# Other rotary groups, and exchanged rows for the layer norm, in a planned two-layer encoder

## The chip, the cores and the metric

The kernel runs on one core of a Trainium2 chip. The metric is the device time of one execution in microseconds (us), taken as the median of several runs. The engines are PE (matrix products; PEld loads their stationary operand), DVE (vector work), ACT (activations and copies), POOL and SP. SP issues almost all DMAs, in the order of its program; POOL issues those that add into memory. Every engine runs its own instructions strictly in the order in which they were written down, so an instruction that waits holds everything behind it on that engine.

## The reference

Two layers over 512 positions of width 1024. Each layer has a token mixer and a squared-ReLU MLP, and each of these four sub-layers is wrapped alike (shift, scale and gate come from the conditioning vector c):

```python
h = x * (1 + scale) + shift
x = layer_norm(DN_ALPHA * x + (1 + gate) * f(h), ln_g, ln_b)
```

The mixer of layer 0 is windowed attention with 8 query heads and 2 key heads (head h uses key head h // 4), with rotary embedding on the first 32 of 128 dimensions:

```python
qkv = h @ w_in
q, k = partial_rope(q, cos, sin), partial_rope(k, cos, sin)
scores = einsum(qb, kb) * HEAD_DIM ** -0.5        # band of 3 blocks of 128
probs = softmax with a sink logit per head
o = einsum(probs, vb) @ w_out
```

The mixer of layer 1 is a recurrent block.

## The kernel before, in words

The kernel is written as a list of operations in program order (`Program.add`). Then `Program.schedule` plans them: it runs through time with a cost for each operation, keeps for each engine the operations whose inputs are done, and takes the one of lowest priority number (its place in the list, shifted by hand-set offsets). What comes out is one fixed order for each engine, and the eight PSUM banks are dealt out along with it. So a change in what waits for what changes the order of many instructions, not only of those in the diff. All of them carry line 502 in the profile (500 for the transposes that open a tile); tiles are told apart by name.

Matrix products are done in three passes (`mm3`): every operand is split into a high part and a rest. Weights come from HBM into four buffers `raw`, ACT casts the high part into one of six buffers `w`, and DVE subtracts to get the rest. `hth` and `htl` hold the layer's input, split and transposed.

In `attn`, after the projection, eight PSUM tiles hold k0, k1 and q0 to q5. `rope` takes four of them at a time: ACT copies the first 32 rows of each into a packed 128-row buffer in `rows[4]`, the tiles are copied whole to their places, DVE shuffles, multiplies by the tables of cosines and sines in `rows[2]`, and adds, and SP sends the four rotated pieces back by DMA. It is called for k0, k1, q0, q1, then for q2 to q5, and later for q6 and q7, always with `rows[4]`. The names of the copies in memory: k0 and k1 are `hid_106` and `hid_107`, q0 is in `exa`, q1 in `ex_73` (profile: `ex`), q3 in `ex_74`, q4 in `exb`, q5 in `ex_75` (profile: `ex`).

Then come the heads in the order 0, 5, 1, 2, 3, 4, 6, 7 (function `head`): four score products, a masking step with a maximum on DVE, exponentials on ACT, normalising, ten transposes on PE, copies, four products with V. Between the heads' instructions PE does the late projection of q6 and q7 (`w_91`, `w_92`) and the first output products.

Behind all this run the background products with the conditioning weights (`gemv_tasks`): `exc`, `hida` and, later, `htl` and `exa`, `exb` are loaded with 128 rows of a weight, scaled and summed over eight such loads. In the first of these products every other load is scaled on ACT and added by a DMA that POOL issues (`rows<-exc`); the others are added on DVE. A buffer is loaded anew when its rows have been added.

`load_ln_rows` loads the layer norm's g into `rows[1]` and b into `rows[2]`. `mod_rows` multiplies (1 + scale) by g into `rows[3]` and scales g and b by alpha. `evac` adds an output tile to x, `ln_block` normalises a block of 128 positions, transposes it, and at the end multiplies x by g on DVE and adds b by a DMA from POOL. Memory is shared: `rows[0]` holds c until the projection is done and the gate row later; `rows[1]` also holds two of the eight score buffers of the heads (`srings`) and, in the first MLP, every other sum of the background products; `rows[2]` also holds the rotary table; in the recurrent block both are parts of larger buffers.

Of the kernel before, what the change touches and what calls it, by code (L numbers as in the profile page):

```python
# [12 lines left out]
ALU = mybir.AluOpType  # L13
# [538 lines left out]
class Kernel:  # L552
# [143 lines left out]
    def fill(self):  # L696
# [17 lines left out]
        QE='aavavavava',  # L714
# [100 lines left out]

    def load_ln_rows(self, i):
        nc = self.nc
        nc.sync.dma_start(out=self.rows[1][:, :], in_=self.I["lng"][i].partition_broadcast(128))
        nc.sync.dma_start(out=self.rows[2][:, :], in_=self.I["lnb"][i].partition_broadcast(128))

    def mod_rows(self, ln, shift, scale):

        nc, v = self.nc, self.nc.vector
        r = self.rows
        v.scalar_tensor_tensor(out=r[3][:, :], in0=r[3][:, :], scalar=1.0, in1=r[1][:, :], op0=ALU.add, op1=ALU.mult)
        for i in (1, 2):
            nc.scalar.activation(out=r[i][:, :], in_=r[i][:, :], func=AF.Copy, scale=ALPHA)
        self.renew("ex", (8, 9))
        sel, tmp = r[4][0:36, 0:512], [self.acc2[0:4, i * 256 : i * 256 + 256] for i in range(3)]
        nc.sync.dma_start(out=sel, in_=self.I["sel"])  # L830
        nc.scalar.copy(out=self.ex[9][0:36, :].bitcast(F32R), in_=sel)
        nc.sync.dma_start(out=tmp[0], in_=self.I["lnb4"][ln])
        for i, row in ((1, scale), (2, shift)):
            nc.sync.dma_start(out=tmp[i].rearrange("p (f c) -> p f c", f=2), in_=self.mods[row][0:1, :].quarters())
        v.scalar_tensor_tensor(out=tmp[1], in0=tmp[1], scalar=1.0, in1=tmp[0], op0=ALU.add, op1=ALU.mult)
        v.tensor_tensor(out=tmp[2], in0=tmp[2], in1=tmp[1], op=ALU.add)
        nc.gpsimd.memset(self.ex[8][0:36, 0:256], 0.0)
        nc.scalar.copy(out=self.ex[8][0:4, 0:256].bitcast(F32R), in_=tmp[2])
        v.tensor_tensor(out=self.ex[8][32:36, 0:256].bitcast(F32R), in0=tmp[2], in1=self.ex[8][0:4, 0:256], op=ALU.subtract)
# [23 lines left out]
    def ln_block(self, t, last=False, parts=1):  # L863
        nc = self.nc
        v = nc.vector
        end = last and t == TB - 1
        near = last and t == TB - 2
        xs = self.xb[t][:, :]
        mv = self.small("mv", 8)
        v.bn_aggr(out=mv[:, 0:2], in_=self.st[t][:, :].rearrange("p (a b) -> p a b", a=2 * parts))  # L870
        nc.scalar.activation(out=mv[:, 2:3], in_=mv[:, 1:2], func=AF.Sqrt, bias=self.eps[:, 0:1])
        v.tensor_scalar(out=mv[:, 3:4], in0=mv[:, 1:2], scalar1=EPS, scalar2=None, op0=ALU.add)
        v.reciprocal(out=mv[:, 4:5], in_=mv[:, 2:3])
        if not end:
            v.scalar_tensor_tensor(out=mv[:, 7:8], in0=mv[:, 0:1], scalar=-1.0, in1=mv[:, 4:5], op0=ALU.mult, op1=ALU.mult)
        v.scalar_tensor_tensor(out=mv[:, 5:6], in0=mv[:, 4:5], scalar=mv[:, 3:4], in1=mv[:, 4:5], op0=ALU.mult, op1=ALU.mult)
        v.tensor_scalar(out=mv[:, 5:6], in0=mv[:, 5:6], scalar1=-0.5, scalar2=1.5, op0=ALU.mult, op1=ALU.add)
        v.tensor_tensor(out=mv[:, 6:7], in0=mv[:, 4:5], in1=mv[:, 5:6], op=ALU.mult)
        mu, rstd = mv[:, 0:1], mv[:, 6:7]
        if not end:  # L880
            v.tensor_tensor(out=mv[:, 7:8], in0=mv[:, 7:8], in1=mv[:, 5:6], op=ALU.mult)
        for fh in range(2):
            c = slice(fh * 512, fh * 512 + 512)
            xh = xs[:, c]
            u = self.ex[8 + 2 * (t & 1) + fh][:, :]
            h = self.ex[4 * (t & 1) + 2 * fh][:, :]
            if end or near and not fh:
                v.scalar_tensor_tensor(out=u, in0=xh, scalar=mu, in1=self.rows[1][:, c], op0=ALU.subtract, op1=ALU.mult)
                w = 256 if end and fh else 512
                for i in range(0, 512, w):  # L890
                    b = slice(fh * 512 + i, fh * 512 + i + w)
                    v.scalar_tensor_tensor(
                        out=h[:, i : i + w], in0=u[:, i : i + w], scalar=rstd, in1=self.rows[2][:, b], op0=ALU.mult, op1=ALU.add
                    )
                    nc.sync.dma_start(out=self.O[t * 128 : t * 128 + 128, b], in_=h[:, i : i + w])
            elif last:
                nc.scalar.activation(out=xh, in_=xh, func=AF.Identity, scale=rstd, bias=mv[:, 7:8])
                nc.gpsimd.tensor_tensor(out=u, in0=xh, in1=self.rows[1][:, c], op=ALU.mult)
                nc.gpsimd.tensor_tensor(out=h, in0=u, in1=self.rows[2][:, c], op=ALU.add)
                nc.sync.dma_start(out=self.O[t * 128 : t * 128 + 128, c], in_=h)  # L900
            else:
                nc.scalar.activation(out=xh, in_=xh, func=AF.Identity, scale=rstd, bias=mv[:, 7:8])
                v.tensor_tensor(out=h, in0=xh, in1=self.rows[3][:, c], op=ALU.mult)
            if last:
                continue
            pt = self.ps()
            for j in range(4):
                nc.tensor.transpose(pt[:, j * 128 : j * 128 + 128], h[:, j * 128 : j * 128 + 128], self.ident[:, :], start=j == 0)
            bm, sel = self.ex[8][0:36, fh * 128 : fh * 128 + 128].bitcast(F32R), self.ex[9][0:36, :].bitcast(F32R)
            nc.tensor.matmul(pt[:, :], lhsT=bm, rhs=sel, start=False, stop=True, skip_group_check=True)  # L910
            a = fh * 2048
            hv, lv = (x[:, a : a + 2048].rearrange("p (k n) -> p k n", k=4)[:, :, t * 128 : t * 128 + 128] for x in self.ht)
            pv = pt[:, :].rearrange("p (k n) -> p k n", k=4)
            if self.par("LE") == "v":
                self.split(pv, hv.bitcast(F32R), lv.bitcast(F32R))
            else:
                uv = u.rearrange("p (k n) -> p k n", k=4)
                nc.scalar.copy(out=hv.bitcast(F32R), in_=pv)
                nc.scalar.copy(out=uv, in_=pv)
                nc.gpsimd.tensor_tensor(out=lv.bitcast(F32R), in0=uv, in1=hv, op=ALU.subtract)  # L920
        if not last:
            self.nc.offset += self.par("XO")
            e = v if self.par("XE") == "v" else nc.gpsimd
            e.tensor_tensor(out=xs, in0=xs, in1=self.rows[1][:, :], op=ALU.mult)
            nc.gpsimd.dma_start(out=xs, in_=self.rows[2][:, :], accum_op=ALU.add)
            self.nc.offset -= self.par("XO")

    def warm_sqrt(self):
# [109 lines left out]
        nc.sync.dma_start(out=self.rows[2][:, :], in_=I["rope"].rearrange("p a b -> p (a b)"))  # L1038
        nc.sync.dma_start(out=self.ex[12][:, 0:384], in_=I["mask"])

    def rope(self, heads, how):

        nc, v = self.nc, self.nc.vector
        n = 32 * len(heads)
        cos, sin = self.rows[2][:n, 0:512], self.rows[2][:n, 512:1024]
        pk, sw = self.rows[4][:n, 0:512], self.rows[4][:n, 512:1024]
        for i, (p, dst) in enumerate(heads):
            nc.scalar.copy(out=self.rows[4][32 * i : 32 * i + 32, 0:512], in_=p[0:32, :])
        for i, (p, dst) in enumerate(heads):
            if how[i] == "a":  # L1050
                nc.scalar.copy(out=dst, in_=p[:, :])
            else:
                v.tensor_copy(out=dst, in_=p[:, :])
        v.stream_shuffle(out=sw, in_=pk, mask=[(i + 16) % 32 for i in range(32)])
        v.tensor_tensor(out=pk, in0=pk, in1=cos, op=ALU.mult)
        v.tensor_tensor(out=sw, in0=sw, in1=sin, op=ALU.mult)
        v.tensor_tensor(out=pk, in0=pk, in1=sw, op=ALU.add)
        for i, (p, dst) in enumerate(heads):
            nc.sync.dma_start(out=dst[0:32, :], in_=self.rows[4][32 * i : 32 * i + 32, 0:512])

    def attn(self):
        nc, I = self.nc, self.I
        v = nc.vector
# [12 lines left out]
        def KTt(kv, lo, hi):  # L1076
            return hid[8 + kv][:, lo:hi]
# [86 lines left out]
        self.own = self.big[:2]  # L1164
        self.modes = self.P["AM"]
        qk = [(tiles[m], KTt(m, 0, 512) if m < 2 else Q(m - 2, 0, 512)) for m in range(8)]
        self.rope(qk[:4], self.P["QE"][:4])
        self.rope(qk[4:], self.P["QE"][4:8])
        accv, r = self.acc2, [a[:, :] for a in self.rows]
        self.bgq += self.gemv_tasks(0, 2, r[3], self.rows[0], red="pe", ap=self.P["AP0"])  # L1170
        self.bgq += self.gemv_tasks(1, 1, accv, self.rows[3], red="pe", ap=self.P["AP1"])
# [2 lines left out]
        u = N_WQ  # L1174
        self.prep(u + 1, ahead=2)
        self.nc.offset += self.P["VP"]
        for t in range(TB):
            p = self.ps()
# [15 lines left out]
        for n in range(2):  # L1194
            u = N_WQ + 2 + n
            self.prep(u, ahead=2)
            p = self.ps()
# [405 lines left out]
```

## Time and profile before

| | us |
|---|---|
| median of 3 runs (1181.89 to 1183.45) | 1182.77 |
| time of the profiled execution | 1187.53 |
| span of its trace | 1185.7 |
| PE busy in that span | 1146.8 |
| DVE busy | 822.9 |
| ACT busy | 530.3 |
| mean granted clock of PE | 0.988 |

The trace belongs to one execution, so durations are compared with its own time. A row of the timeline gives start, duration, engine, operation, output and inputs, shape, and in brackets how long the engine was idle before and what ended that. "Granted clock" is the share of PE's full clock that it was given.

### The profile page before, as it was taken

To read this page: it belongs to the slowest core of one execution; us is meant where nothing else is said; L and a number is where in the kernel's file an instruction comes from. 1 tells how busy PE (TensorE), PEld (TensorE's weight loads), DVE (VectorE), ACT (ScalarE), POOL (GpSimd) and SP (SyncE) were. 2 spreads that over 40 slices of the span, in tenths; PEclk is the share of its full clock that TensorE was granted. 3 is DMA by queue.
4 is the path that set the end of the run, shared out by engine and by line. 5 is a ranking of instruction groups with operands and counts; after the bars stand their busy time and mean duration, and the time that the engine had idled before them with its cause. 6 is when DMAs were issued, how large, how long until landed. Compare 5 with 4: busy or idle time off the path is not lost.

```text
span 1185.7 us, 14389 instructions
## 1 busy us (share of the span) xinstructions
PE 1146.8 (97%) x5292; PEld 932.8 (79%) x5292; DVE 822.9 (69%) x1228; ACT 530.3 (45%) x784; POOL 100.6 (8%) x73
## 2 busy tenths in 40 slices
PE   6989999999999999999999999999999999999995
PEld 4876677988888888888887877878988888888884
DVE  8767878898999844448748889799644444444447
ACT  5357554521332522324469989825422422422411
POOL 1000000233222200000000000000000000000004
PEclk9989999999999999999999999999999999999998
DMA  9876754876588332223434464544722223222201
GB/s 347 320 213 184 260 171 127 255 258 246 188 318 313 102 112 89 99 98 74 134 106 127 143 157 125 154 148 140 199 89 100 96 89 107 89 95 101 89 1 72
DMA packets 57369, 181.85 MB, mean 153 GB/s; under 512 B 8017, under 2 KB 8589, under 8 KB 57298
## 3 DMA queue, kind: packets, MB, share of 16 engines
q1 hardware_dynamic: 53698, 170.19, 41.5%
q0 software_dynamic: 3600, 10.75, 4.9%
q8 instruction: 41, 0.67, 0.2%
q14 instruction: 30, 0.25, 0.1%
HBM read 160.29 MB, written 2.13 MB: 137 GB/s over the span
## 4 chain that ended last, share of the span: by engine, by line
PE 70%; DVE 11%; ACT 8%; DMA 7%; issue 3%; SPq 0%; DVEq 0%; ACTq 0%
PE ps L502 69%; DVE w L502 3%; ACT rows L502 3%; DVE rows L502 2%; ACT w L502 2%; ACT L502 1%; DMA rows<-rows 1%; DMA raw<-in_W 1%; DVE ex L502 1%; PE ps L500 1%; DVE acc L502 1%; DVE xb L502 1%; DMA rows<-w 1%; ACT ex L502 1%; ACT acc L502 1%
## 5 line engine op out<-in xcount | busy, mean ns | idle before, releaser
L502 PE MATMUL ps<-hth,w 128*128 128x512 f32 (+1 forms) x1776 | 505.4, 369 | 2.8 <-ACT hth L502 1.8
L502 DVE TENSOR_TENSOR w<-raw,w 128x1024 fp32r<-128x1024 f32 x192 | 236.9, 1238 | 240.5 <-ACT w L502 238.4
L502 ACT CAST w<-raw 128x1024 fp32r<-128x1024 f32 x192 | 198.4, 1040 | 431.0 <-PE ps L502 382.6
L502 PEld LDWEIGHTS ps<-hth,w 128*128 128x128 f32 x1776 | 321.8, 190 | 61.8 <-ACT hth L502 1.9
L502 PE MATMUL ps<-w,hid 128*128 128x512 f32 (+1 forms) x1581 | 368.9, 390 | 0.0
L502 PEld LDWEIGHTS ps<-w,hid 128*128 128x128 f32 x1581 | 295.1, 189 | 64.4 <-issue 0.7
L502 PE MATMUL ps<-htl,w 128*128 128x512 f32 (+1 forms) x888 | 326.8, 368 | 0.0
L502 PEld LDWEIGHTS ps<-htl,w 128*128 128x128 f32 x888 | 168.1, 189 | 29.4 <-issue 0.7
L502 PE MATMUL ps<-w,hth 128*128 128x512 f32 (+1 forms) x256 | 68.4, 373 | 2.8 <-DVE w L502 1.7
L502 DVE SCALAR_TENSOR_TENSOR ex<-rows,ps 128x512 f32<-128x512 f32 (+1 forms) x81 | 53.2, 674 | 13.8 <-PE ps L502 13.7
L502 DVE TENSOR_TENSOR ex<-rows 128x512 f32<-128x512 f32 x64 | 48.6, 761 | 10.8 <-ACT rows L502 10.7
L502 DVE TENSOR_TENSOR xb<-xb,ex 128x512 f32<-128x512 f32 (+1 forms) x81 | 54.9, 694 | 1.4 <-ACT xb L502 0.9
L502 PEld LDWEIGHTS ps<-w,hth 128*128 128x128 f32 x256 | 45.3, 188 | 13.0 <-DVE w L502 2.1
L502 PE MATMUL ps<-w,hida 128*128 128x512 f32 (+1 forms) x219 | 54.2, 388 | 0.0
L502 ACT ACTIVATE rows<-ps 128x512 f32<-128x512 f32 x66 | 39.1, 593 | 25.8 <-PE ps L502 25.8
L502 DVE TENSOR_TENSOR hid<-ex,hid 128x512 fp32r<-128x512 f32 x57 | 45.5, 797 | 3.9
L502 PEld LDWEIGHTS ps<-w,hida 128*128 128x128 f32 x219 | 40.9, 188 | 8.8
L502 ACT ACTIVATE hid<-rows 128x512 fp32r<-128x512 f32 x56 | 35.4, 632 | 1.7
L502 POOL DMA_DIRECT2D xb<-rows x12 | 10.5, 874 | 290.7 <-DVE xb L502 157.4
L502 ACT ACTIVATE xb<-xb,mv 128x512 f32<-128x512 f32 x29 | 22.1, 809 | 29.0 <-DVE mv L502 29.0
L502 ACT ACT_TABLE_LOAD x26 | 33.4, 1283 | 3.2 <-DMA w<-w 2.1
L502 POOL TENSOR_TENSOR ex<-xb,rows 128x512 f32<-128x512 f32 x3 | 3.8, 1286 | 329.5 <-ACT xb L502 329.5
(191 smaller groups left out, 1020.0 us busy)
## 6 DMA issues: line engine op xcount, KB each, us to landing
raw<-in_W SPq DMA_DIRECT2D x184, 512.0 KB
exc<-in_adaw SPq DMA_DIRECT2D x28, 512.0 KB
exa<-in_adaw SPq DMA_DIRECT2D x19, 512.0 KB
exb<-in_adaw SPq DMA_DIRECT2D x18, 512.0 KB
xb<-rows POOLq DMA_DIRECT2D x12, 512.0 KB, 5.3
hida<-in_adaw SPq DMA_DIRECT2D x9, 512.0 KB
ex<-in_ada0t SPq DMA_DIRECT2D x17, 256.0 KB
htl<-in_adaw SPq DMA_DIRECT2D x6, 512.0 KB
```

The costliest lines, as they stand in the source:

```text
L500: op.ins = nc.tensor.matmul(args[0], lhsT=args[1], rhs=args[2], is_transpose=True, stop=False, skip_group_check=True, **kw)
L502: op.ins = getattr(getattr(nc, op.eng), op.fn)(*args, **kw)
```

## The change

Two things. The first call of `rope` takes k0, k1, q0 and q5, with `rows[4]` as before; the second takes q1 to q4 and packs them into `rows[0]`. And g is loaded into `rows[2]`, b into `rows[1]`, with every use of the two following.

```diff
     def load_ln_rows(self, i):
         nc = self.nc
-        nc.sync.dma_start(out=self.rows[1][:, :], in_=self.I["lng"][i].partition_broadcast(128))
-        nc.sync.dma_start(out=self.rows[2][:, :], in_=self.I["lnb"][i].partition_broadcast(128))
+        nc.sync.dma_start(out=self.rows[2][:, :], in_=self.I["lng"][i].partition_broadcast(128))
+        nc.sync.dma_start(out=self.rows[1][:, :], in_=self.I["lnb"][i].partition_broadcast(128))
...
-        v.scalar_tensor_tensor(out=r[3][:, :], in0=r[3][:, :], scalar=1.0, in1=r[1][:, :], op0=ALU.add, op1=ALU.mult)
-        for i in (1, 2):
+        v.scalar_tensor_tensor(out=r[3][:, :], in0=r[3][:, :], scalar=1.0, in1=r[2][:, :], op0=ALU.add, op1=ALU.mult)
+        for i in (2, 1):
...
-            e.tensor_tensor(out=xs, in0=xs, in1=self.rows[1][:, :], op=ALU.mult)
-            nc.gpsimd.dma_start(out=xs, in_=self.rows[2][:, :], accum_op=ALU.add)
+            e.tensor_tensor(out=xs, in0=xs, in1=self.rows[2][:, :], op=ALU.mult)
+            nc.gpsimd.dma_start(out=xs, in_=self.rows[1][:, :], accum_op=ALU.add)
...
-    def rope(self, heads, how):
+    def rope(self, heads, how, at=4):
...
-        pk, sw = self.rows[4][:n, 0:512], self.rows[4][:n, 512:1024]
+        pk, sw = self.rows[at][:n, 0:512], self.rows[at][:n, 512:1024]
...
-        self.rope(qk[:4], self.P["QE"][:4])
-        self.rope(qk[4:], self.P["QE"][4:8])
+        self.rope(qk[:3] + qk[7:], self.P["QE"][:4])
+        self.rope(qk[3:7], self.P["QE"][4:8], 0)
```

The plan comes out differently from the rotary step to the first part of the first MLP; further on only a few row loads and scalings change places. Three places follow, each before and after.

PE, after the V products: `hid_106` and `hid_107` are the keys k0 and k1, `ex_73` is q1, `ex_75` is q5, `w_91` is a weight of the late projection. Before:

```order
L502 MATMUL ps_687<-hid_106,ex_73 128x256
L502 MATMUL ps_691<-hid_106,ex_73 128x384
L502 MATMUL ps_697<-hid_106,ex_73 128x384
L502 MATMUL ps_702<-hid_106,ex_73 128x256
L502 MATMUL ps_705<-hth,w_91 128x512
L502 MATMUL ps_705<-htl,w_91 128x512
L502 MATMUL ps_705<-hth,w_91 128x512 x2
...
L502 MATMUL ps_718<-hid_107,ex_75 128x256
L502 MATMUL ps_720<-hid_107,ex_75 128x384
```

After:

```order
L502 MATMUL ps_684<-hid_106,exa 128x384
L502 MATMUL ps_688<-hid_106,exa 128x256
L502 MATMUL ps_690<-hid_107,ex_75 128x256
L502 MATMUL ps_693<-hid_107,ex_75 128x384
L502 MATMUL ps_696<-hid_107,ex_75 128x384
L502 MATMUL ps_700<-hid_107,ex_75 128x256
L502 MATMUL ps_703<-hid_106,ex_73 128x256
L502 MATMUL ps_707<-hid_106,ex_73 128x384
L502 MATMUL ps_711<-hid_106,ex_73 128x384
L502 MATMUL ps_720<-hid_106,ex_73 128x256
L502 MATMUL ps_722<-hth,w_91 128x512
```

Head 5's scores now come directly behind head 0's; before, head 1's and the first seven matmuls of the late projection stood between.

ACT, the copies out of PSUM after the projection: `ps_190` to `ps_240` are k0, k1, q0 to q5, and `exc` is the first load of the background products. Before:

```order
L502 CAST w_92<-raw_85 128x1024
L502 COPY ex_73<-ps_201 128x512
L502 COPY ex_74<-ps_227 128x512
L502 COPY ex_75<-ps_240 128x512
L502 ACTIVATE exc<-exc,sc 128x1024
L502 CAST w_87<-raw_82 128x1024
L502 COPY hid_109<-ps_537 128x256
L502 CAST w_88<-raw_83 128x1024
L502 COPY hid_110<-ps_573 128x256
L502 COPY rows<-ps_204 32x512
```

After:

```order
L502 CAST w_92<-raw_85 128x1024
L502 COPY rows<-ps_204 32x512
L502 COPY rows<-ps_240 32x512
L502 COPY ex_75<-ps_240 128x512
L502 COPY rows<-ps_227 32x512
L502 COPY rows<-ps_233 32x512
L502 COPY exa<-ps_204 128x512
L502 COPY exb<-ps_233 128x512
L502 CAST w_87<-raw_82 128x1024
L502 CAST w_88<-raw_83 128x1024
L502 COPY hid_109<-ps_536 128x256
L502 ACTIVATE exc<-exc,sc 128x1024
```

The packing of q2 to q5 has moved ahead, and the scaling of `exc` behind it, two casts and a V copy.

SP, the loads at the end of the heads: `rows<-in_lng` is g, `rows<-in_lnb` is b, `xb` are the four blocks of x. Before (b is loaded much earlier, right behind the rows of q6 and q7):

```order
L502 DMA mods_1244<-rows 1x1024
L502 DMA raw_85<-in_W 128x1024
L502 DMA xb_1294<-in_x 128x1024
L502 DMA rows<-in_sel 36x512
L502 DMA raw_82<-in_W 128x1024
L502 DMA rows<-in_lng 128x1024
L502 DMA mods_1327<-acc_69 1x1024
L502 DMA xb_1332<-in_x 128x1024
```

After (g is in that earlier place):

```order
L502 DMA mods_1254<-rows 1x1024
L502 DMA rows<-in_lnb 128x1024
L502 DMA xb_1279<-in_x 128x1024
L502 DMA xb_1287<-in_x 128x1024
L502 DMA xb_1291<-in_x 128x1024
L502 DMA xb_1296<-in_x 128x1024
L502 DMA raw_85<-in_W 128x1024
L502 DMA rows<-in_sel 36x512
```

The late row is now b, and it stands ahead of all four blocks of x and of two weight loads.

More of the change, by code (lines that the diff above doesn't have):

```diff
@@ L887, in ln_block @@
             if end or near and not fh:
-                v.scalar_tensor_tensor(out=u, in0=xh, scalar=mu, in1=self.rows[1][:, c], op0=ALU.subtract, op1=ALU.mult)
+                v.scalar_tensor_tensor(out=u, in0=xh, scalar=mu, in1=self.rows[2][:, c], op0=ALU.subtract, op1=ALU.mult)
                 w = 256 if end and fh else 512
@@ L892, in ln_block @@
                     v.scalar_tensor_tensor(
-                        out=h[:, i : i + w], in0=u[:, i : i + w], scalar=rstd, in1=self.rows[2][:, b], op0=ALU.mult, op1=ALU.add
+                        out=h[:, i : i + w], in0=u[:, i : i + w], scalar=rstd, in1=self.rows[1][:, b], op0=ALU.mult, op1=ALU.add
                     )
@@ L897, in ln_block @@
                 nc.scalar.activation(out=xh, in_=xh, func=AF.Identity, scale=rstd, bias=mv[:, 7:8])
-                nc.gpsimd.tensor_tensor(out=u, in0=xh, in1=self.rows[1][:, c], op=ALU.mult)
-                nc.gpsimd.tensor_tensor(out=h, in0=u, in1=self.rows[2][:, c], op=ALU.add)
+                nc.gpsimd.tensor_tensor(out=u, in0=xh, in1=self.rows[2][:, c], op=ALU.mult)
+                nc.gpsimd.tensor_tensor(out=h, in0=u, in1=self.rows[1][:, c], op=ALU.add)
                 nc.sync.dma_start(out=self.O[t * 128 : t * 128 + 128, c], in_=h)
@@ L1045, in rope @@
         cos, sin = self.rows[2][:n, 0:512], self.rows[2][:n, 512:1024]
-        pk, sw = self.rows[4][:n, 0:512], self.rows[4][:n, 512:1024]
+        pk, sw = self.rows[at][:n, 0:512], self.rows[at][:n, 512:1024]
         for i, (p, dst) in enumerate(heads):
-            nc.scalar.copy(out=self.rows[4][32 * i : 32 * i + 32, 0:512], in_=p[0:32, :])
+            nc.scalar.copy(out=self.rows[at][32 * i : 32 * i + 32, 0:512], in_=p[0:32, :])
         for i, (p, dst) in enumerate(heads):
@@ L1058, in rope @@
         for i, (p, dst) in enumerate(heads):
-            nc.sync.dma_start(out=dst[0:32, :], in_=self.rows[4][32 * i : 32 * i + 32, 0:512])
+            nc.sync.dma_start(out=dst[0:32, :], in_=self.rows[at][32 * i : 32 * i + 32, 0:512])
     def attn(self):
```

## The prediction

> **What bounds the kernel now.** I read the page first: the shares of the engines and the chain that ended last.
>
> ```profile
> span 1185.7 us, 14389 instructions
> PE 1146.8 (97%) x5292; PEld 932.8 (79%) x5292; DVE 822.9 (69%) x1228; ACT 530.3 (45%) x784; POOL 100.6 (8%) x73
> PE 70%; DVE 11%; ACT 8%; DMA 7%; issue 3%; SPq 0%; DVEq 0%; ACTq 0%
> ```
>
> PE is busy for 97% of the span and has 70% of the chain. The change adds and removes no matmul, so it can only win where PE waits or runs at a lower clock. The instruction order (below) shows which stretches it touches: from the rotary step, at about 57 us, to the first quarter of the first MLP. From there on PE's order is the same. So next I read the windows of that stretch; the columns are the stretch, its length, busy time of PE, PEld, DVE, ACT and POOL, the granted clock, and the DMA share.
>
> ```profile
> 72.00:83.00 11.00, 6.68 (x28) 4.45 (x26) 6.95 (x16) 7.49 (x16) 0.87 (x1) 0.94 0.92 280
> 83.00:95.00 12.00, 12.00 (x43) 8.70 (x44) 7.10 (x24) 5.28 (x12) 0.00 (x0) 0.77 0.34 103
> 95.00:160.00 65.00, 62.77 (x271) 43.97 (x270) 54.78 (x116) 43.04 (x107) 2.66 (x3) 1.00 0.68 222
> 185.00:215.00 30.00, 29.74 (x181) 24.49 (x181) 25.53 (x52) 13.56 (x21) 3.91 (x5) 0.94 0.61 161
> ```
>
> PE is idle for 4.3 us in the first and 2.2 us in the third. In the second it is busy throughout, but 23% of its clock is withheld: 0.23 x 12 = 2.8 us. In the last it is 0.06 x 30 = 1.8 us. PE's timeline and the transfers name the waits:
>
> ```profile
> 72.26 2.31 PE L502 MATMUL ps<-hid,exa 128*128 128x256 f32 x8
> 77.48 0.50 PE L502 MATMUL ps<-hth,w 128*128 128x512 f32 x1 [0.75 <-DVE mx L502]
> 82.93 4.61 PE L502 MATMUL ps<-hid,ex 128*128 128x256 f32 x8 [3.57 <-issue]
> 90.60 0.38 PE L502 MATMUL ps<-ident,xb 128*128 128x128 f32 x2
> 77.73 0.59 SPq L502 DMA_DIRECT2D ex<-rows  x1
> 66.14 4.64 DMA exa<-rows
> ```
>
> At 72.26 head 0's scores start, at 90.60 its first transposes. Between them PE stands for 3.57 us before head 5's scores (82.93). Head 5's query is q5, whose rotary rows went out last of the second group, on SP at 77.73; another row DMA of that kind took 4.64 us (the chain's row at 66.14), so these landed at about 82.4. The wait is for q5.
>
> The second place is the first layer norm.
>
> ```profile
> 159.91 0.27 PE L502 MATMUL ps<-ident,rows 128*128 128x128 f32 x1
> 160.21 5.62 DMA rows<-in_lng
> 165.92 1.23 DVE L502 SCALAR_TENSOR_TENSOR rows<-rows 128x1024 f32<-128x1024 f32 x1 [1.97 <-DMA rows<-in_lng]
> 167.18 1.06 ACT L502 ACTIVATE rows<-rows 128x1024 f32<-128x1024 f32 x1 [3.96 <-DVE rows L502]
> 170.03 2.01 ACT L502 ACTIVATE xb<-xb 128x1024 f32<-128x1024 f32 x2
> 167.35 2.27 PE L502 MATMUL ps<-w,hid 128*128 128x512 f32 x9
> 169.45 1.55 PE L502 MATMUL ps<-w,hth 128*128 128x512 f32 x6
> 185.00 0.63 PE L500 MATMUL ps<-ident,exa 128*128 128x128 f32 x4 [1.17 <-DVE exa L502]
> ```
>
> The last head's transposes read `rows[1]` at 159.91; only then may g be loaded into it. DVE waits for g (165.92), ACT behind DVE (167.18), the evacuations behind both, and PE stands 1.17 us for the first normalised block (185.00).
>
> **Part one, the rotary groups.** With q5 in the first group, head 5's scores follow head 0's, and seven late projection matmuls no longer come between. The 3.57 us go, and with them the low clock behind them, 2.8 us: 6.3 us, if PE's next work is ready. It isn't quite.
>
> ```profile
> 57.95 1.78 ACT L502 COPY rows<-ps 32x512 f32<-32x512 f32 x3
> 61.66 1.57 ACT L502 COPY ex<-ps 128x512 f32<-128x512 f32 x3
> 63.10 1.19 ACT L502 ACTIVATE exc<-exc,sc 128x1024 f32<-128x1024 f32 x1
> 64.15 1.08 ACT L502 CAST w<-raw 128x1024 fp32r<-128x1024 f32 x1
> 70.87 1.18 ACT L502 COPY rows<-ps 32x512 f32<-32x512 f32 x2 [1.30 <-DMA exa<-rows]
> 70.59 1.28 DVE L502 SCALAR_TENSOR_TENSOR rows<-hida,sc,rows 128x1024 f32<-128x1024 f32 x1 [2.88 <-DMA rows<-exc]
> 70.58 0.33 SPq L502 DMA_DIRECT2D exc<-in_adaw  x1
> 75.34 1.15 ACT L502 ACTIVATE exc<-exc,sc 128x1024 f32<-128x1024 f32 x1 [0.74 <-DMA exc<-in_adaw]
> 79.14 0.30 ACT L502 ACTIVATE es<-nm,sinks 128x4 f32<-128x4 f32 x1 [1.35 <-DVE nm L502]
> 81.43 0.19 ACT L502 ACTIVATION_READ_ACCUMULATOR ex<-ex,nm 128x1 f32 x1
> 89.19 0.15 DVE L502 TENSOR_TENSOR den<-den,es 128x4 f32<-128x4 f32 x1
> ```
>
> Before, the second group's packing waited on ACT for the first group's row DMAs (70.87). Now it doesn't, so four row copies and all of the head copies are drawn ahead of the first gate-row scaling `exc`, with two weight casts and one V copy. By their rows (0.59, 0.53 and about 1.0 us apiece, the V copy, half as wide as a head's, put at 0.3) that scaling starts at 61.7 + 4 x 0.59 + 3 x 0.53 + 2 x 1.0 + 0.3 = 67.9 us, 4.8 us later than 63.10; 61.66 is where the copies after the last common cast began. Everything in its loop moves along: its add by DMA landed at 70.5 (DVE's wait at 70.59), SP reloaded `exc` at 70.58, ACT could scale again at 75.34. Now that second scaling comes at about 80.1, and on ACT it stands ahead of head 0's exponentials. These began 3.8 us after it (79.14), of which 1.35 were a wait for DVE that is over by then: 80.1 + 2.5 = 82.6. They take until 82.6 + 2.5 = 85.1 (79.14 to 81.62). From the sum on DVE (89.19) to the transposes (90.60) it was 1.4 us: 86.5 instead of 90.60.
>
> PE is there by then or soon after: three heads' scores (2.3 us each) from 72.26 end at 79.2, and 18 matmuls at 0.233 us (167.35 to 169.45 for 9) end at 83.4, or at 87.6 with the whole burst at half clock. So head 0's transposes come 4.1 us earlier, with one matmul less done (0.2): 3.9. The bounds are 2.8 (half clock) and 6.3 (nothing waits). Head 5's transposes then find ACT still busy with head 0's copies and a cast; I give back 0.7 us, between 0 and the 1.2 of one such scaling. Net **-3.2 us**. What could cost here and is covered is on DVE:
>
> ```profile
> L502 DVE TENSOR_TENSOR w<-raw,w 128x1024 fp32r<-128x1024 f32 x192 | 236.9, 1238 | 240.5 <-ACT w L502 238.4
> ```
>
> The first group's shuffle now stands behind one more weight step (1.2 us), so its rows go out that much later and `exa` lands at 72.0 instead of 70.8; PE wants it at 72.26. If that cover is gone, PE waits for the difference, and a wait of a few tenths is what I would expect at worst. On SP the rows of q1 to q4 go out behind one weight load; head 1's scores, third on PE, want q1 at 72.26 + 2 x 2.3 = 76.9, so its rows must leave by 72.3, and packing that no longer waits (70.87) allows that.
>
> **Part two, g and b.** `rows[2]` is free after the last rotary group, so g loads during the heads and the multiplication by it no longer holds the evacuations: 1.97 + 1.23 = 3.2 us of the chain. PE's order puts the first transposes 6 matmuls (1.4 us) earlier. 3.2 - 1.4 covers the 1.17 us wait with 0.6 to spare. Now b is the late row: SP holds it until the last head's transposes, and all four loads of x stand behind it. From 159.91 the last x was scaled at 172.04, 12.1 us. But PE's order now has 50 matmuls (11.7 us), not 21, and the last head's product between these transposes and the end of the first output half, so x is ready about there. I take -1.17 and -1.8 for the clock behind it: **-3.0 us**, between 0 and -3.0.
>
> The half clock is taken from these rows: 1.17 us of waiting, then
>
> ```profile
> 187.00:188.00 1.00, 1.00 (x4) 0.87 (x4) 0.70 (x2) 0.59 (x1) 0.60 (x1) 0.70 0.00 0
> 190.00:191.00 1.00, 1.00 (x5) 0.77 (x4) 0.68 (x3) 0.52 (x1) 0.00 (x0) 0.59 1.02 197
> ```
>
> a clock below 1 from 187 to 191 with PE busy. The Trainium skill, "TensorE: Matmul & The Clock Gate", section "Why this matters for your kernels", says that PE falls back to half clock after a wait of over some 3 us. The trace has the fall after 1.17 us; by that rule the 1.8 us would stay and part two be worth 1.2 us.
>
> **Where the rows swap later.**
>
> ```profile
> 777.62 0.33 SPq L502 DMA_DIRECT2D rows<-in_lnb  x1
> 781.37 1.06 ACT L502 ACTIVATE rows<-rows 128x1024 f32<-128x1024 f32 x1 [0.21 <-DMA rows<-in_lnb]
> 783.90 1.22 DVE L502 SCALAR_TENSOR_TENSOR rows<-rows 128x1024 f32<-128x1024 f32 x1
> 220.04 0.33 SPq L502 DMA_DIRECT2D rows<-in_lnb  x1
> 231.80 3.26 DVE L502 SCALAR_TENSOR_TENSOR rows<-exb,sc,rows 128x1024 f32<-128x1024 f32 x1
> ```
>
> After the recurrent block `rows[2]` comes free later than `rows[1]`; g now goes out at 777.62 in b's place and lands at 781.3, the multiplication begins at 783.90: nothing, with 2.5 us in reserve. In the first MLP `rows[1]` is a sum row of the background products. It must now wait for the adds of b, which ended before 220.04 (b's load waited for them); a clearing and a bias load follow, and the first sum in it was at 231.80: nothing.
>
> **The sum.** -3.2 - 3.0 = -6.2 us. The profiled execution, 1187.53 us by its own time (span 1185.7), becomes 1181.3. It ran 4.8 us above the median of the three runs, 1182.77; against that the forecast is 1182.77 - 6.2 = **1176.6 us**.
>
> **Rivals.**
> - One gain only: the heads give theirs back later, or the layer norm still waits. 1182.77 - 3.1 = 1179.7. For it: DVE has 54.8 of 65 us in the heads, so little is idle.
> - The clock behind 185.00 falls for another reason and stays: -4.4, 1178.4. Against it: the clock is 1.00 from 95 to 160, where no such wait stands, and fell behind both longer ones. This is what the skill's rule would make of it.
> - Nothing: q5's place is taken by the scaling on ACT, landing some 4 us later than I count, and b takes g's: 1182.8.
> - Slower: DVE becomes the bound of the heads. The new order ends the heads 29 matmuls (6.8 us) earlier in PE's stream, and DVE's idle time there is 10.2 us, of which PE's earlier arrival takes 3 to 4. If DVE holds PE at the transposes of the six later heads, each wait of 1.17 us costs 1.8 more in clock, 3.0 us; the third takes -6.2 to +2.8: 1185.6. It decides from the third such wait on. Against it: no wait of PE between 95 and 160 lowered the clock, and the sums of the background products moved behind the heads in DVE's order.
>
> **How the numbers follow.** Forecast 0.52 (its own range 1174 to 1179.5), one gain 0.18, the clock 0.05, nothing 0.12, slower 0.13. The low end: all idle time and lost clock of the four windows (4.3 + 2.8 + 2.2 + 0.3 + 1.8) and the 1.17 make 12.6, so 1170.2 is the floor; I put 1171. The high end, 1183.5, takes in "nothing" and leaves out most of "slower". A measurement of this kernel can tell 0.2% (2.4 us) from no change. Faster by more: the forecast, the clock case and 0.13 of "one gain", 0.70. Within: 0.05 + 0.12 = 0.17. Slower: 0.13.
>
> **What would show it.** Right: head 5's scores directly behind head 0's on PE, no wait of over 1 us and no clock of 0.5 for 5 us in 79 to 89; `exc` scaled near 68 and 80; head 0's transposes near 86.5; DVE's multiplication by g without a wait for its load; PE's first transposes of the layer norm without a wait, and a clock of 1.00 behind them. Wrong: transposes of head 0 near 90, or waits of over 1 us before several heads' transposes with half clock behind each, or ACT waiting for b.

## The result, and the profile after

The changed kernel is slower: 1191.66 us (median of 5 runs, 1188.02 to 1192.43) against 1183.45 us in the same job, a ratio of 1.0054 (95% interval 1.0028 to 1.0080). A second job gave 1190.67 us and 1.0043 (1.0019 to 1.0066). Three executions in all the jobs (1418 us of the kernel before, 1523 of swap_first_norm below, 2929 of the changed kernel) lay far above the rest and are left out of every ratio. The forecast was 1176.6 us. The profiled execution took 1192.43 us, with a span of 1190.7.

The page after, span and busy time; before, PE had the same work in a span 5 us shorter:

```profile
span 1190.7 us, 14377 instructions
PE 1147.0 (96%) x5292; PEld 934.0 (78%) x5292; DVE 821.9 (69%) x1228; ACT 530.6 (45%) x784; POOL 100.8 (8%) x73
```

The windows of the changed stretch (columns as in the prediction; the last two are the first MLP's beginning):

```profile
72.00:83.00 11.00, 8.82 (x35) 6.18 (x34) 7.48 (x21) 4.58 (x8) 0.87 (x1) 1.00 0.95 286
83.00:95.00 12.00, 11.29 (x53) 7.65 (x52) 8.83 (x25) 10.92 (x30) 0.85 (x1) 1.00 0.56 151
95.00:160.00 65.00, 62.48 (x266) 43.85 (x265) 52.08 (x109) 43.24 (x101) 1.81 (x2) 1.00 0.78 253
185.00:215.00 30.00, 29.10 (x211) 25.71 (x210) 23.20 (x42) 13.05 (x19) 2.57 (x3) 1.00 0.74 199
215.00:240.00 25.00, 21.19 (x129) 18.61 (x128) 23.92 (x25) 11.18 (x16) 9.26 (x4) 1.00 0.63 205
240.00:262.00 22.00, 20.78 (x84) 16.95 (x85) 21.05 (x17) 6.37 (x7) 8.31 (x3) 0.92 0.85 309
```

In these windows of the heads and of the layer norm the clock is 1.00, and PE is idle for 2.2 us in the first window where it was 4.3. But from 215 to 240 us, where PE had been busy for all 25 us, it now stands for 3.8. PE's timeline names the places:

```profile
74.04 2.75 PE L502 MATMUL ps<-hid,ex 128*128 128x256 f32 x10
78.96 1.99 PE L502 MATMUL ps<-hid,ex 128*128 128x384 f32 x6 [2.17 <-DVE mx L502]
85.51 0.44 PE L502 MATMUL ps<-ident,xb 128*128 128x128 f32 x2 [0.43 <-DVE xb L502]
178.31 0.66 PE L500 MATMUL ps<-ident,exa 128*128 128x128 f32 x4
204.12 0.63 PE L500 MATMUL ps<-ident,exb 128*128 128x128 f32 x4 [0.90 <-DVE exb L502]
235.11 1.08 PE L502 MATMUL ps<-w,hid 128*128 128x512 f32 x4
241.22 1.00 PE L502 MATMUL ps<-hth,w 128*128 128x512 f32 x2 [5.04 <-DVE w L502]
571.29 0.63 PE L500 MATMUL ps<-ident,exb 128*128 128x128 f32 x4 [1.66 <-DVE exb L502]
```

Head 0's transposes stand at 85.51 (before 90.60), the layer norm's first at 178.31 without a wait (before 185.00 with 1.17 us), its last at 204.12; before, these stood at 211.68, as this row shows, and those of the second layer norm at 571.15:

```profile
211.68 0.55 PE L500 MATMUL ps<-ident,exb 128*128 128x128 f32 x3 [0.25 <-DVE exb L502]
571.15 0.63 PE L500 MATMUL ps<-ident,exb 128*128 128x128 f32 x4 [1.66 <-DVE exb L502]
```

One sign that the prediction had named for being wrong did appear: ACT waited 3.93 us for b. PE lost nothing by it, as its first transposes (178.31) show.

```profile
153.29 1.06 ACT L502 ACTIVATE rows<-rows 128x1024 f32<-128x1024 f32 x1 [3.93 <-DMA rows<-in_lnb]
```

So this execution was 7.6 us ahead when the first MLP began and level when it ended. The wait at 241.22 is for DVE's half of a weight, in the eighth tile of that MLP: PE has done the tile's first 2 matmuls and, at 235.11, four of the next product, and 22 of the tile are left. In the kernel before, the tile was done in one go, ahead of that product. DVE's timeline after, from the first sum in `rows[1]` on:

```profile
224.45 1.29 DVE L502 SCALAR_TENSOR_TENSOR rows<-exb,sc,rows 128x1024 f32<-128x1024 f32 x1 [0.99 <-DMA exb<-in_adaw]
225.65 2.73 DVE L502 TENSOR_TENSOR hid<-ex,hid 128x512 fp32r<-128x512 f32 x1
228.31 3.33 DVE L502 TENSOR_TENSOR ex<-rows 128x512 f32<-128x512 f32 x2
...
233.37 1.27 DVE L502 SCALAR_TENSOR_TENSOR rows<-exc,sc,rows 128x1024 f32<-128x1024 f32 x1
...
235.17 1.27 DVE L502 SCALAR_TENSOR_TENSOR rows<-exa,sc,rows 128x1024 f32<-128x1024 f32 x1
...
236.97 1.27 DVE L502 SCALAR_TENSOR_TENSOR rows<-exb,sc,rows 128x1024 f32<-128x1024 f32 x1
...
238.76 1.27 DVE L502 SCALAR_TENSOR_TENSOR rows<-exc,sc,rows 128x1024 f32<-128x1024 f32 x1
239.96 4.62 DVE L502 TENSOR_TENSOR w<-raw,w 128x1024 fp32r<-128x1024 f32 x4
```

And before:

```profile
227.44 1.22 DVE L502 TENSOR_TENSOR w<-raw,w 128x1024 fp32r<-128x1024 f32 x1
```

There the weight step came at 227.44, ahead of the first of these sums (231.80). After, five sums, none of which PE needs, stand in front of it, 5 x 1.27 = 6.4 us of DVE, and it comes at 239.96. POOL adds to that: while its two reductions run, one DVE instruction at 225.65 and one of the two at 228.31 are 2 us longer each. In the kernel before, the reductions fell behind that weight step, on the instructions at 231.80 (3.26 us) and 234.98. POOL's lines after show why the row is late: it is cleared only when the last add of b has landed, 10 us after that add was issued.

```profile
206.38 0.86 POOL L502 DMA_DIRECT2D xb<-rows  x1 [4.84 <-DVE xb L502]
216.14 0.95 POOL L502 MEMSET rows<- 128x1024 f32 x1 [8.90 <-DMA xb<-rows]
```

### The profile page after: what moved, and what is told of

It reads as the page before. It is cut to its first block, busy times and chain, and to the rows that moved or that the text cites. A ratio compares the mean times of both kernels' runs of the same rounds, so it can differ in the third digit from the quotient of the medians.

```text
span 1190.7 us, 14377 instructions
## 1 busy us (share of the span) xinstructions
PE 1147.0 (96%) x5292; PEld 934.0 (78%) x5292; DVE 821.9 (69%) x1228; ACT 530.6 (45%) x784; POOL 100.8 (8%) x73
## 4 chain that ended last, share of the span: by engine, by line
PE 73%; DVE 9%; DMA 8%; ACT 7%; issue 2%; SPq 0%; POOL 0%; DVEq 0%; ACTq 0%; POOLq 0%
PE ps L502 72%; DVE w L502 3%; ACT rows L502 2%; DMA rows<-rows 2%; ACT w L502 2%; DVE ex L502 1%; DVE rows L502 1%; DMA rows<-exc 1%; PE ps L500 1%; DMA exc<-in_adaw 1%; ACT L502 1%; DMA exb<-in_adaw 1%; DVE acc L502 1%; DMA rows<-w 1%; DVE exb L502 1%
## 5 line engine op out<-in xcount | busy, mean ns | idle before, releaser
L502 DVE TENSOR_TENSOR ex<-rows 128x512 f32<-128x512 f32 x64 | 53.5, 837 | 14.4 <-ACT rows L502 14.4
```

The costliest lines, as they stand in the source:

```text
L502: op.ins = getattr(getattr(nc, op.eng), op.fn)(*args, **kw)
```

## The experiments

Theory A: the gain in front is real and is lost in the first MLP, where the sum row, now the row of b, is late, so that the plan puts sums ahead of a weight step. Rival B: whatever comes early is lost there anyway. Rival C: the rows that swap behind the recurrent block cost the time. All ratios are to the kernel before in the same job; its median was 1183.45 to 1184.86 in them. Verdicts rest on ratios, since one kernel's executions spread over some 12 us (1180 to 1192 for the kernel before).

| kernel | median us | ratio (95% interval) |
|---|---|---|
| rope_only | 1185.66 | 1.0008 (0.9991 to 1.0026) |
| swap_only | 1193.80 | 1.0072 (1.0044 to 1.0100) |
| sum_row_2 | 1185.30 | 1.0005 (0.9987 to 1.0023) |
| swap_first_norm | 1183.47 | 0.9994 (0.9978 to 1.0011) |
| before_sum_in_b | 1191.10 | 1.0057 (1.0034 to 1.0080) |
| weights_first | 1180.77 | 0.9969 (0.9951 to 0.9987) |
| norm0_weights_first | 1179.95 | 0.9963 (0.9950 to 0.9976) |
| before_weights_first | 1183.94 | 0.9990 (0.9975 to 1.0004) |
| rope_weights_first | 1182.39 | 0.9972 (0.9955 to 0.9989) |
| swap_weights_first | 1188.51 | 1.0021 (1.0004 to 1.0039) |
| groups_only | 1181.04 | 0.9968 (0.9949 to 0.9986) |
| buffer_only | 1183.46 | 0.9983 (0.9963 to 1.0003) |
| old_rows_behind | 1189.84 | 1.0036 (1.0015 to 1.0057) |
| changed_again | 1190.67 | 1.0043 (1.0019 to 1.0066) |

### Each part alone, and the sum row moved

rope_only is the kernel before with the change's two `rope` calls and the new argument; swap_only is the changed kernel with the old calls.

> The kernel before with the new rotary groups alone; g and b stay where they were, so the sums of the first MLP lie in the row that g leaves. Theory A (the gain in front is real, and it was lost in the first MLP because the sum row waits for the adds of b and pushes a weight step behind the sums): head 0's transposes near 85.5 us, no PE wait of over 2 us in the first MLP, and 3 to 6 us below the kernel before. Rival B (what comes early is lost anyway, since weight loads or the background products set the pace of the first MLP): head 0's transposes early too, but a new PE wait of 3 to 4 us in the first MLP and a time within 2 us of before. Rival C (most of the loss comes from the rows that change places behind the recurrent block): faster by 3 to 6 us, as A.

> The changed kernel with the old rotary groups: g and b in exchanged rows, nothing else. Theory A: the layer norm gains 1 to 3 us, the first MLP loses 4 to 8 as the sum row waits for the adds of b; 3 to 7 us above the kernel before, with a PE wait of over 3 us in the first MLP. Rival B: the layer norm's gain is lost, nothing more: within 2 us of before. Rival C: the first MLP is as before and the loss of some 5 us comes between 730 and 830 us.

rope_only: head 0's transposes at 85.52, no wait of over 1.5 us in the first MLP, but no gain in the median. The profile was of a lucky execution (1182.56 us). swap_only: slower, by as much as the whole change. The price was A's, the place was not: its layer norm gained nothing (a wait of 1.93 us at 183.37 and one of 1.56 at 202.48), and in the first MLP the longest wait was 1.46 us, not the 3 that A said. Its sum row is the row of b and was cleared late too (222.64 us), but DVE had the weight step after only two sums (231.33 and 241.45, the step at 242.65). So a late row need not bring the bunch, and what swap_only lost in its first MLP is not shown.

sum_row_2 is the changed kernel with

```diff
-        accs, red = (self.acc2, self.rows[1][:, :]), self.ex[8:10]
+        accs, red = (self.acc2, self.rows[2][:, :]), self.ex[8:10]
```

> The changed kernel with one row moved: the second sum row of the background products in the first MLP is the row of g, not the row of b. Theory A: the PE wait of 5 us at 241 us is gone and with it 7 to 8 us: 1182 to 1185 us if the later stages still lose their 5 us, 1177 to 1180 us if those were chance. Rival B: the wait stays, at 3 to 5 us, for a weight whose load comes too late; within 2 us of the changed kernel (1190 to 1192). Rival C: as A, with the loss between 730 and 830 us still there: 1184.

The wait of 5.04 us shrank to 1.07, and the loss went from 1.0054 to 1.0005; the weight step stands ahead of the first sum in the row again (224.95 and 233.93 us): A. Yet nothing was gained over before, which left room for B. swap_first_norm adds to this that g and b go back from the second layer norm on (all users follow):

```diff
     def load_ln_rows(self, i):
+        if i:
+            self.gb_at = 1, 2
+        g, b = self.gb_at
-        nc.sync.dma_start(out=self.rows[2][:, :], in_=self.I["lng"][i].partition_broadcast(128))
-        nc.sync.dma_start(out=self.rows[1][:, :], in_=self.I["lnb"][i].partition_broadcast(128))
+        nc.sync.dma_start(out=self.rows[g][:, :], in_=self.I["lng"][i].partition_broadcast(128))
+        nc.sync.dma_start(out=self.rows[b][:, :], in_=self.I["lnb"][i].partition_broadcast(128))
```

> As the kernel with the sums in the row of g, but g and b go back to their old rows from the second layer norm on, so that the rows behind the recurrent block load as before. Theory A: the same time as with the sum row alone moved, within 1.5 us. Rival C: 3 to 5 us faster than that. Rival B: no faster than the changed kernel.

It came out 1.8 us lower in the median, with overlapping intervals: neither theory gains by it.

### The fault alone, and its order alone

before_sum_in_b is the kernel before with the same one-line edit as sum_row_2: there `rows[2]` is the row of b.

> The kernel before, with its old rotary groups and its old rows for g and b, and one thing changed: the second sum row of the first MLP lies in the row of b. So it has the suspected fault alone. Theory A (a sum row that waits for the adds of b makes the plan put four sums ahead of a weight step, and PE waits for that step): a PE wait of 3 to 6 us between 230 and 250 us, 5 to 8 us above the kernel before. Rival B (the first MLP loses only what came early): no such wait, within 2 us of before, since nothing comes early here. Rival D (the loss belongs to the rotary groups' new plan as a whole): within 2 us of before.

A. The wait before the eighth tile appears in a kernel that has neither new groups nor exchanged rows:

```profile
246.35 1.03 PE L502 MATMUL ps<-hth,w 128*128 128x512 f32 x2 [4.16 <-DVE w L502]
```

weights_first leaves the rows of the changed kernel alone and gives the weight steps of the first MLP a lower number in the planner (`conv_unit` adds this offset):

```diff
-        CO=(-50, 150, 150),
+        CO=(-50, 50, 150),
```

> The changed kernel with its rows as they are (sums in the row of b); the weight steps of the first MLP get an earlier place (offset 50 instead of 150), so that they stand ahead of the sums on DVE. Theory A in its stricter form (the order on DVE is what costs, not that the row comes late): no PE wait of over 2 us in the first MLP, 6 to 8 us below the changed kernel, 1182 to 1185. Rival A2 (the late row itself holds up SP and the weight loads queued behind its bias load): a wait of 3 us or more stays, 1188 to 1192.

The stricter form of A holds. The sum row is still as late (cleared at 215.22, its bias loaded at 216.21), but from 215 us on five weight steps now stand ahead of its first sum on DVE (239.38), where the changed kernel has one, and PE does not wait:

```profile
215.00:240.00 25.00, 25.00 (x145) 21.95 (x144) 22.82 (x24) 12.70 (x18) 8.73 (x4) 1.00 0.59 194
240.00:262.00 22.00, 22.00 (x98) 18.04 (x97) 19.43 (x17) 5.74 (x8) 4.47 (x2) 1.00 0.93 337
```

So it is the order on DVE that cost, and A2 is refuted. B, as a law of the first MLP, is refuted too: with these steps first, the changed kernel is 0.31% faster than before. norm0_weights_first and before_weights_first make the same edit in swap_first_norm and in the kernel before:

> The version with g and b exchanged in the first layer norm only and the sums in the row of g, with the weight steps of the first MLP at the earlier place as well. In its profile without that, PE waited 1.12 us at 204 us, 0.8 at 241 and 1.46 at 404 us, in the first MLP, the last two for weight steps. If the gain in front of 3 us is only lost in these waits: 1.5 to 3 us below that version, 1180.5 to 1182, so 2 to 4 below the kernel before. If later stages take up whatever comes early (rival B moved to the recurrent block, whose ACT is busy for 45 of 50 us from 690 to 740): 1183 to 1184.5, no gain.

> The kernel before with the weight steps of the first MLP at the earlier place: the control for the two others. Its own trace has a single PE wait in the first MLP, of 0.26 us, so nothing is to be gained: within 1.5 us of before. If it gains as much as the version of the first norm does, the earlier place is worth something by itself.

The first has the lowest ratio found, 0.37% below before, though its interval overlaps with others; the control gains nothing that can be told from zero. The control has the same offset and is the fairer measure: weights_first against it, in the same job, is 1180.77 to 1183.94 us, a ratio of 0.9973, and the means differ by 2.2 us, give or take 2.0.

The earlier place mends more than the fault. These are the last transposes of the first and of the second layer norm in sum_row_2, then in weights_first:

```profile
204.74 0.63 PE L500 MATMUL ps<-ident,exb 128*128 128x128 f32 x4 [1.12 <-DVE exb L502]
567.52 0.63 PE L500 MATMUL ps<-ident,exb 128*128 128x128 f32 x4 [1.66 <-DVE exb L502]
203.44 0.63 PE L500 MATMUL ps<-ident,exb 128*128 128x128 f32 x4 [1.43 <-DVE exb L502]
563.74 0.63 PE L500 MATMUL ps<-ident,exb 128*128 128x128 f32 x4 [1.66 <-DVE exb L502]
```

So the stretch between them is 362.8 us in sum_row_2, 360.3 in weights_first, 359.5 in the kernel before, and 367.2 in the changed kernel, of which 1.7 are clock. Of the 7.7 us that the change lost there, 4.4 are the fault with its clock; some 3 are lost without it (362.5 us in rope_only too), in part in waits for weight steps (1.07 and 1.46 us in sum_row_2, 1.46 in rope_only), and the earlier place brings most of them back. With the old offset B is right in kind for these 3 us. These are single profiles.

### Which part brings the gain

rope_weights_first and swap_weights_first are rope_only and swap_only with that edit. groups_only and buffer_only are rope_weights_first with, in turn,

```diff
-        self.rope(qk[3:7], self.P["QE"][4:8], 0)
+        self.rope(qk[3:7], self.P["QE"][4:8])
```

```diff
-        self.rope(qk[:3] + qk[7:], self.P["QE"][:4])
-        self.rope(qk[3:7], self.P["QE"][4:8], 0)
+        self.rope(qk[:4], self.P["QE"][:4])
+        self.rope(qk[4:], self.P["QE"][4:8], 0)
```

> The kernel before with the new rotary groups, g and b in their old rows, and the weight steps of the first MLP at the earlier place, so that the fault in the first MLP is absent: what the rotary groups are worth by themselves. By the prediction's two terms (3.2 for the heads, 3.0 for the layer norm): 3.2 below the kernel before, 1181.5. Theory E (the rotary groups alone bring both terms, because the last head ends 29 matmuls earlier and with it the load of g; with them alone the trace showed no PE wait at the layer norm's first transposes): 4 to 5 below, 1180 to 1181, as much as with both parts.

> The kernel before with g and b in exchanged rows and the weight steps of the first MLP at the earlier place: what the exchange is worth by itself. By the prediction's terms: 3 below the kernel before, 1181.5. Theory E (the exchange brings nothing: with it alone PE still waited 1.93 us for the first normalised block, since b took the place of g and x was scaled behind it): no PE wait over 2 us in the first MLP, the wait at the first transposes still 1 to 2 us, 1183 to 1185.

> As the rotary groups with the weight steps first, but both groups packed in the one buffer: k0, k1, q0, q5 and then q1 to q4, the second packing waiting for the first group's DMAs. If the place of q5 is what counts (the prediction's reason: the 3.57 us before head 5's scores): no such wait, head 0's transposes near 86, 3 to 4 us below the kernel before. If the second buffer is what counts: head 1's or head 0's work waits 2 to 4 us, within 2 us of before.

> As the rotary groups with the weight steps first, but with the old groups (k0, k1, q0, q1 and q2 to q5), the second packed in a buffer of its own. If the place of q5 is what counts: its rows leave last of the second group still, head 5's scores wait 2 to 3 us, within 2 us of before. If the second buffer is what counts: q5 is there in time, since the packing no longer waits for the first group's DMAs, head 0's transposes near 86, 3 to 5 us below the kernel before.

The rotary groups alone give 0.9972, as much as both parts (0.9969): theory E in kind, though 3.3 us is less than its 4 to 5. The exchange alone is slower even with the weights first, by more than E or the prediction's terms foresaw (1188.51 us). In its trace PE waits four times from the first layer norm to the first MLP's start, 5.0 us in all:

```profile
183.33 0.63 PE L500 MATMUL ps<-ident,exa 128*128 128x128 f32 x4 [1.62 <-DVE exa L502]
194.84 0.39 PE L502 MATMUL ps<-htl,w 128*128 128x256 f32 x1 [0.47 <-DVE htl L502]
199.37 0.66 PE L500 MATMUL ps<-ident,exa 128*128 128x128 f32 x4 [1.55 <-DVE exa L502]
208.46 0.63 PE L500 MATMUL ps<-ident,exb 128*128 128x128 f32 x4 [1.38 <-DVE exb L502]
```

ACT in swap_only, which has the same wait at its first transposes (1.93 us), shows the reason for the first: b is now the load that is waited for, and x, loaded behind it, is scaled as late as before, until 170.41, 12.1 us after the last head's transposes (158.28).

```profile
164.53 1.06 ACT L502 ACTIVATE rows<-rows 128x1024 f32<-128x1024 f32 x1 [2.76 <-DMA rows<-in_lnb]
166.51 1.06 ACT L502 ACTIVATE xb<-xb 128x1024 f32<-128x1024 f32 x1 [0.92 <-DMA xb<-in_x]
168.41 2.00 ACT L502 ACTIVATE xb<-xb 128x1024 f32<-128x1024 f32 x2
```

With the new groups the last head ends earlier, and then even the late row, here g in rope_only on DVE, holds nobody up:

```profile
151.24 1.23 DVE L502 SCALAR_TENSOR_TENSOR rows<-rows 128x1024 f32<-128x1024 f32 x1 [0.61 <-DMA rows<-in_lng]
177.86 0.60 PE L500 MATMUL ps<-ident,exa 128*128 128x128 f32 x4
```

Of the two edits in the groups, q5's place alone (groups_only) gives 0.9968 and the second buffer alone 0.9983, whose interval just reaches 1. In both plans head 5's scores follow head 0's. groups_only waits 1.25 us for q1's rows and buffer_only 1.86 us before head 5; the 3.57 us are gone in either, and head 0's transposes come early in both (87.09 and 85.44). So by the traces either edit does most of it; by the times only the place of q5 has a gain that is shown, and with overlapping intervals the share of the second buffer stays open.

### What was lost behind the first MLP

The first profile of the change lost 5 us behind the first MLP too. old_rows_behind is the changed kernel with the old rows from the second layer norm on (the fault in the first MLP kept); changed_again is the changed kernel.

> The changed kernel with its fault in the first MLP (sums in the row of b), but g and b back in their old rows from the second layer norm on. In the profiled execution of the changed kernel some 5 us were lost behind the first MLP. Rival C (the rows that change places there cost them): 3 to 5 us below the changed kernel, 1186 to 1188, the PE wait before the eighth tile still 4 to 5 us. If they were chance of that execution, from the clock's windows and a DMA in the recurrent block: the same as the changed kernel within 2 us, 1189 to 1192.

> The changed kernel itself, for a second profile and more times beside the kernel with the old rows behind. The wait before the eighth tile of the first MLP should be there again, 4.5 to 5.5 us, and half clock behind it or not as the windows fall. If the 5 us behind the first MLP were chance, another part of them is lost this time: the waits at the recurrent block's end (3.7 and 0.8 us in the first profile) differ by over 1 us; if they belong to the change, they come again, with half clock behind. Time 1189 to 1192.

C is refuted: the two differ by 0.8 us, and the wait before the eighth tile is there in both, 4.57 and 5.62 us. The wait at the recurrent block's end, 3.73 us in the first profile of the change, is 3.12 in the second; it came again, against my reading as chance. It does not belong to the change alone either: rope_only has 3.47 there, the kernel before 0.58. But it is not what cost the 5 us. From the second layer norm's last transposes to PE's last product the profiles of before, of the change, of the change again and of the old rows take 601.7, 607.1, 604.6 and 604.1 us, and there the clock was at half for 10.2, 20.5, 17.1 and 17.1 us. Half of that is lost work if PE is busy in it; without it the stretches are 596.6, 596.9, 596.1 and 595.6 us. So the loss behind the first MLP was the clock.

## Why the prediction was wrong

**The step that failed** is "In the first MLP ... nothing". It asked when the late row could be cleared and loaded, and found that early enough for its first sum. So it was (cleared at 216.14 us, first sum at 224.45). It did not ask what stands behind the sums on DVE: five of them ahead of a weight step, for which PE waited 5.04 us. Its remark "From there on PE's order is the same" is no help: in the traces it holds from about 336 us on, and the wait lies ahead of that, in the stretch that the change touches, where PE's order changed as well (235.11). The sums are background work that nobody waits for; they hurt because of the weight step behind them. That a late row lets several sums come due together in the plan, with lower numbers than that step, is argued from the planner's rule; the plan's own times are not shown. Shown is that the bunch comes with the row (before_sum_in_b) and goes with it (sum_row_2). The fault cost 0.57% in before_sum_in_b and 0.4 to 0.5% between the changed kernel and sum_row_2, 5 to 7 us with the clock behind it. Another 0.36% lies between sum_row_2 and weights_first: the early start was also lost in smaller waits, on which the prediction is silent.

**The heads** went as worked out, nearly number for number: `exc` was scaled at 67.49 and 79.71 us (forecast 67.9 and 80.1), head 0's exponentials began at 82.18 (82.6), its transposes at 85.51 (86.5). The wait for q5 went; a wait of 2.17 us for DVE's maxima took part of its place, not foreseen, but PE would have been early for the transposes anyway.

**The layer norm's term had the wrong owner.** The -3.0 was credited to the exchange, because DVE waited 1.97 us for g. The exchange alone left the wait (1.93 us in swap_only), since b and x then came as late as g had. What removed it was the rotary groups: the earlier end of the last head, which the prediction knew (29 matmuls) and used only for a rival. A load that is waited for is late for a reason; moving another load into its place moves the lateness.

**The sum.** -6.2 us against, with the fault taken out, a ratio of 0.9969, which is -3.7 us (-1.5 to -5.8), and 0.9973 or -3.2 us against the control: the right sign, and a little over half the size. In the single profiles the lead is still 5 to 7 us at the second layer norm (last transposes at 563.74 us in weights_first, 569.10 in before_weights_first, 571.15 in before). What takes the rest behind it, beyond the draws of the clock, the runs do not settle.

**The rivals.** "Slower" was given 0.13 for a reason that did not occur: DVE does not bound the six later heads, where PE stood for 2.5 us from 95 to 160 us, before for 2.2. Slower came by a DVE wait 80 us further on, in a stage that the prediction had closed.

**The clock.** The sum takes 1.8 us of it at the layer norm, with a chance of 0.05 against, and the heads' 90.60 us, from which it counts, holds the 2.8. It is a draw in each execution. The last transposes of the second layer norm are preceded by the same wait of 1.66 us in before, after and rope_only (at 571.15, 571.29 and 566.18 us). The windows behind it, before:

```profile
571.00:574.00 3.00, 2.85 (x14) 2.06 (x15) 2.65 (x5) 1.17 (x2) 0.51 (x1) 0.85 0.01 0
574.00:577.00 3.00, 3.00 (x15) 2.71 (x15) 0.56 (x1) 0.00 (x0) 0.35 (x1) 0.58 0.78 153
577.00:580.00 3.00, 3.00 (x28) 3.00 (x27) 1.24 (x2) 1.41 (x2) 0.00 (x0) 1.00 0.12 22
```

After:

```profile
571.00:574.00 3.00, 2.71 (x11) 1.57 (x12) 2.67 (x4) 0.84 (x3) 0.36 (x1) 0.77 0.01 0
574.00:577.00 3.00, 3.00 (x12) 2.71 (x13) 0.69 (x1) 0.46 (x1) 0.50 (x1) 0.50 0.72 141
577.00:580.00 3.00, 3.00 (x18) 3.00 (x18) 0.00 (x0) 0.50 (x1) 0.00 (x0) 0.59 0.18 34
```

And in rope_only:

```profile
566.00:569.00 3.00, 2.82 (x15) 1.99 (x16) 2.64 (x5) 1.19 (x3) 0.47 (x1) 1.00 0.01 0
569.00:572.00 3.00, 3.00 (x27) 2.96 (x26) 0.60 (x1) 0.83 (x2) 0.38 (x1) 1.00 0.78 152
```

The eighth column is the granted clock. What it withholds is (0.15 + 0.42) x 3 = 1.7 us, then (0.23 + 0.50 + 0.41) x 3 = 3.4 us, then nothing, for one and the same wait. So a term for the clock read from one execution is one draw, and the profiled execution of before, 4.8 us above its median, was an unlucky one. Over the four jobs of the experiments the mean granted clock of the kernel before was 0.98975 (116 runs), and over its two jobs that of the changed one 0.98619 (16 runs), 0.00356 x 1190 = 4.2 us: in each of the four profiles with the long wait before the eighth tile, half clock followed it for 3.4 or 6.8 us. Whether that is all of the 4.2 us stays open.

## What to carry to other kernels

When a buffer that a background task writes changes its owner, look at every engine's order around that task's first use, not at the one that bounds the kernel: late background work can come due in a bunch, and the cost is what waits behind the bunch. Before crediting a wait to the load that it names, ask what would arrive next if that load were early, and test each edit alone. A clock term taken from one trace belongs in the range, not in the sum.

## What the runs showed of the hardware

- In all sixteen traces, from the heads to PE's last product, the stretches of half clock last 3.41 or 6.83 us, and within one execution they start on a grid of 3.41 us, which lies differently in each execution. That is the window that the Trainium skill, "TensorE: Matmul & The Clock Gate", section "What's actually happening", calls free-running; here the traces agree. The same section ties the fall to a whole idle window; here it came also behind windows in which PE had stood for only 1.0 to 1.9 us of the 3.41 (1.01 in the one that ends at 187 us in the kernel before), and failed to come behind others with as much (1.91 in the one that ends at 238 us after). From 60 us to PE's last product of the sixteen traces it came behind every window with 2.0 us or more, and never began behind one with under 1.0. In rope_only the grid's border falls inside the wait before 566.18, so that neither window has over 0.9 us of it; but in norm0_weights_first the same wait lies within one window and nothing followed.
- While POOL's two reductions over partitions run (224.74 to 232.1 us after), one DVE instruction with two operands in memory takes 2.73 us in each (225.65, and one of the two at 228.31) where it took 0.68; another between them took 0.68. In the kernel before, two instructions caught it in the same way (231.80, 3.26 us instead of 1.28, and 234.98); in weights_first the weight step itself did, 3.27 us instead of 1.22, and harmed nobody.
